# A value loop whose VectorE order is written out, with gathers issued five steps ahead

## The chip, the cores and the metric

The kernel runs on one core of a Trainium2 chip. The metric is device time in microseconds (us), as the median of three runs. Profiled spans come from one further execution.

## What is computed

The reference is one layer of a hybrid encoder block on 512 tokens of width 1024: a convolution branch and a windowed attention branch are gated, merged and added to x; then comes a retrieval layer over 16384 single-neuron experts, and a final norm. The change lies in the retrieval layer, so only that is shown, cut to what matters:

```python
for hc in four chunks of 128 tokens:                     # hc: (128, 1024), after RMSNorm
    q  = (hc @ w_query).reshape(128, 8, 2, 128)
    sc = einsum('thpd,pnd->thpn', q, sub_keys)
    vals, idx = top_k(sc, 16)                            # two half keys per head
    expert_idx, gate = top 16 of the 16 x 16 sums, softmax over them
    u   = expert_u[expert_idx]                           # 8 heads x 16 = 128 rows a token
    act = gelu(einsum('thkd,td->thk', u, hc))
    vv  = expert_v[expert_idx]
    y   = einsum('thk,thkd->td', gate * act, vv)
out = rmsnorm(x + y)
```

## The kernel before

The three later token chunks (384 tokens) are worked densely. For each of 128 blocks of 128 experts, `u_block(i)` (lines 491 to 506) loads a 512 KB block of transposed `expert_u` (tile `uraw`), splits it into a high and a low part (`uhi` on ScalarE, `ulo` on GpSimd, two halves a block, line 60), multiplies it with the tokens in 24 matmuls (`hps`, lines 65 to 67) and applies Gelu (line 504, tile `hb`). `v_block(i)` (lines 758 to 763) is the value side. It first calls `v_prep(i + 1)`, which prepares the next block: a load of `expert_v` (`vraw`, line 737, two buffers), its split (`vhl`: high half on ScalarE, low half on VectorE), the product of `hb` with the gates (line 747, VectorE, gates in `gt`, one load for four blocks), and the split of that product (`ph` on ScalarE, `pl` on VectorE, three buffers each). Then 18 matmuls add block i into six PSUM accumulators (`acc`).

Chunk 0 (128 tokens) is worked sparsely: its 128 chosen rows of `expert_u`, then its 128 rows of `expert_v`, are gathered one row per token by an indirect DMA from GpSimd's queue (`gather`, line 701, tile `row`, five buffers, 512 KB each). `step(c)` for c below 128 multiplies gathered rows of u with the tokens and sums (line 708); for c from 128 on it adds a weighted row of v to `yacc` (line 719). Each step is one long VectorE instruction.

The value loop (lines 815 to 824) weaves both. It runs i from 10 to 124. For i up to 91 an iteration has a v block, u block i + 36 and about 2.67 steps; from 92 on (33 iterations) no u block is left and an iteration has a v block and about 1.13 steps. These shares are the constants `R_BOTH` and `R_ONE`. The last three v blocks (125 to 127) follow the loop: blocks 126 and 127 are prepared, then the matmuls run token chunk by token chunk, each chunk followed by `finish`, which adds the residual, norms and stores. `finish(0)` takes `yacc` and stands just ahead of them (line 827).

Each engine works through its own queue in order. The order within a queue comes from the scheduler at build time, which simulates the program and takes, on each engine, what it holds ready, by program priority. Where `tc.manual_schedule` names an engine, that engine's queue keeps the program's order instead. Before the change it names GpSimd alone (line 815): its queue holds, per iteration, the two `ulo` of the u block and then the gathers of that iteration's steps. VectorE's order is the scheduler's. ScalarE, SyncE (which issues the loads) and TensorE are ordered by the scheduler in both kernels.

Of the kernel before, what the change touches and what calls it, by code (L numbers as in the profile page):

```python
# [27 lines left out]
NKEY = 128  # L28
# [7 lines left out]
VB, PB, VR, GB = 4, 3, 2, 5  # L36
UQ, UB = 2, 4
LAST = 3
# [8 lines left out]
def encoder_block(ctx, tc, x, xT, g1, w_in, taps, dwb, lng, lnb, w_pw, sink, w_o, w_out, g2, g2row,  # L47
# [443 lines left out]
    def u_block(i):  # L491
        raw = ust.tile([P, KD, P], F32, name="uraw", bufs=2)
        SP.dma_start(raw.rearrange("p k c -> p (k c)"), ut[i])
        ps = psh.tile([P, TB], F32, name="hps")
        for q in range(UQ):
            n = KD // UQ
            ks = slice(q * n, (q + 1) * n)
            hi = ust.tile([P, n, P], F32R, name="uhi", bufs=UB)
            lo = ust.tile([P, n, P], F32R, name="ulo", bufs=UB)
            split(hi, lo, raw[:, ks, :], POOL)  # L500
            mm3(ps, [(hi[:, k, :], lo[:, k, :]) for k in range(n)],
                [(h2_hi[:, q * n + k, P:], h2_lo[:, q * n + k, P:]) for k in range(n)], q == 0, q == UQ - 1)
        hb = hring.tile([P, TB], F32, name="hb")
        ACT.activation(hb, ps, AF.Gelu)  # L504
        hblk[i] = hb
# [193 lines left out]
    def gather(table, c):  # L699
        row = gath.tile([P, D], F32, name="row")  # L700
        POOL.indirect_dma_start(out=row, out_offset=None, in_=table,  # L701
                                in_offset=bass.IndirectOffsetOnAxis(ap=eidx[:, c:c + 1], axis=0))
        return row

    def step(c):
        if c < NKEY:
            row = gather(u, c)
            DVE.scalar_tensor_tensor(row, row, 1.0, h2tok, op0=OP.mult, op1=OP.mult,  # L708
                                     accum_out=dots[:, c:c + 1])
            if c == NKEY - 1:  # L710
                ACT.activation(dots, dots, AF.Gelu)
                DVE.tensor_tensor(dots, dots, gate_w, op=OP.mult)
        else:
            c -= NKEY
            row = gather(v, c)
            if c == 0:
                DVE.tensor_scalar(yacc, row, dots[:, 0:1], None, op0=OP.mult)
            else:
                DVE.scalar_tensor_tensor(yacc, row, dots[:, c:c + 1], yacc, op0=OP.mult, op1=OP.add)  # L719
# [38 lines left out]
    def v_block(i):  # L758
        v_prep(i + 1)
        for t in range(NB):  # L760
            for hf in range(2):
                v_mm(i, t, hf)
        prepped.pop(i)
# [48 lines left out]
    done, c = 0.0, 0  # L812
    both_n = NKEY - LEAD - NP
    unit = 2.0 * NKEY / (both_n * R_BOTH + (NKEY - NP - both_n) * R_ONE - 4)
    with tc.manual_schedule(engines={mybir.EngineType.Pool}):
        for i in range(NP, NKEY - LAST):
            v_block(i)
            both = i + LEAD < NKEY
            if both:
                u_block(i + LEAD)  # L820
            done += unit * (R_BOTH if both else R_ONE)
            while c < 2 * NKEY and (c < done or i == NKEY - LAST - 1):
                step(c)
                c += 1
    gfint = vst.tile([P, D], F32, name="h2tok", bufs=1)
    SP.dma_start(gfint, bcast(gfin, D))
# [76 lines left out]
```

## Time and profile before

| | us |
|---|---|
| median of three runs | 1776.07 |
| lowest and highest run | 1769.18 and 1780.47 |
| the profiled execution | 1779.59 |
| its span, first to last instruction | 1777.8 |
| busy: TensorE, VectorE, GpSimd, ScalarE | 1723.7, 1425.5, 945.5, 777.7 |
| mean granted TensorE clock | 0.989 of full |

The profiled execution is 1.8 us longer than its span, and 3.5 us longer than the median. Line numbers such as L60 are lines of the kernel; the helper `split` puts all its low parts on L60 and its high parts on L59, so they are told apart by tile. PE is TensorE's matmuls, PEld its weight loads, DVE VectorE, ACT ScalarE, POOL GpSimd, SP SyncE. "idle before" is the engine's idle time just ahead of an instruction and what ended it.

### The profile page before, as it was taken

Reading aid. Unit: us, or ns where it says so; the run is one execution under the profiler, and the core shown is the slowest. Engines: PE = TensorE matmul, PEld = TensorE weight load, DVE = VectorE, ACT = ScalarE, POOL = GpSimd, SP = SyncE. Lnnn points to the kernel's source line nnn. Section 1 sums busy time; section 2 is a strip of 40 time slices with the busy share of each in tenths; the row PEclk is TensorE's granted clock in tenths of the full one; section 3 lists DMA queues with packets and bytes.
Section 4 is the critical chain, followed back from the end, with each engine's and each line's share of the span. In section 5 each row is a group of like instructions: output and inputs, shape, how many; then the busy total and the mean of one; then the engine's idle time right before and its main releaser. Section 6 shows DMA issues by size and latency. Waiting matters only on the chain.

```text
span 1777.8 us, 25338 instructions
## 1 busy us (share of the span) xinstructions
PE 1723.7 (97%) x8843; PEld 1487.6 (84%) x8843; DVE 1425.5 (80%) x2523; ACT 777.7 (44%) x1386; POOL 945.5 (53%) x745
## 2 busy tenths in 40 slices
PE   7999999989999979999999999999999999998998
PEld 6888876668888878998999999999999988997786
DVE  7999967674437999999668888888878768898964
ACT  5333368972253336665433333333433332332343
POOL 6544420020135444445358888878876677786401
PEclk9999999999999989999999999999999999999999
DMA  4232210043243125987879998988997888899952
GB/s 160 98 102 97 95 39 33 13 148 101 83 149 105 45 65 162 285 259 245 311 256 312 328 317 307 328 320 316 319 326 278 314 303 294 304 329 333 357 204 93
DMA packets 158976, 379.44 MB, mean 213 GB/s; under 512 B 12592, under 2 KB 64832, under 8 KB 158848
## 3 DMA queue, kind: packets, MB, share of 16 engines
q1 hardware_dynamic: 120720, 241.73, 38.9%
q0 software_dynamic: 37120, 134.52, 22.0%
q10 hardware_dynamic: 1008, 1.58, 0.3%
q8 instruction: 69, 1.13, 0.3%
q14 instruction: 59, 0.48, 0.1%
HBM read 346.84 MB, written 30.93 MB: 212 GB/s over the span
## 4 chain that ended last, share of the span: by engine, by line
PE 63%; DVE 13%; DMA 12%; issue 6%; POOL 3%; ACT 2%; SPq 0%; ACTq 0%; POOLq 0%; DVEq 0%
PE mm L65 7%; PE mm L67 7%; PE mm L66 7%; PE acc L67 6%; PE acc L66 6%; PE acc L65 6%; PE hps L66 6%; PE hps L65 6%; PE hps L67 5%; DMA row<-in_v_dram,eidx 5%; DMA uraw<-in_ut_dram 3%; DMA vraw<-in_v_dram 2%; PE s L65 2%; POOL row L701 1%; PE s L66 1%
## 5 line engine op out<-in xcount | busy, mean ns | idle before, releaser
L60 POOL TENSOR_TENSOR ulo<-uraw,uhi 128x512 fp32r<-128x512 f32 x256 | 400.7, 1581 | 306.6 <-ACT uhi L59 278.7
L67 PE MATMUL hps<-big,ulo 128*128 128x384 f32 x1024 | 349.0, 341 | 3.6 <-POOL ulo L60 3.6
L65 PE MATMUL hps<-big,uhi 128*128 128x384 f32 x1024 | 348.8, 341 | 2.2 <-ACT hb L504 2.1
L66 PE MATMUL hps<-big,uhi 128*128 128x384 f32 x1024 | 347.5, 339 | 0.0
L67 PE MATMUL acc<-vhl,pl 128*128 128x512 f32 x768 | 301.7, 393 | 8.0 <-DVE pl L60 8.0
L65 PE MATMUL acc<-vhl,ph 128*128 128x512 f32 x768 | 301.3, 392 | 3.6 <-ACT vhl L59 3.5
L66 PE MATMUL acc<-vhl,ph 128*128 128x512 f32 x768 | 301.7, 393 | 0.9 <-DVE vhl L60 0.9
L60 POOL TENSOR_TENSOR wlo<-wraw,whi 128x512 fp32r<-128x512 f32 x120 | 160.8, 1344 | 176.4 <-ACT whi L59 153.6
L708 DVE SCALAR_TENSOR_TENSOR row<-row,h2tok 128x1024 f32<-128x1024 f32 x128 | 206.0, 1610 | 58.3 <-DMA row<-in_u_dram,eidx 56.5
L719 DVE SCALAR_TENSOR_TENSOR yacc<-row,dots,yacc 128x1024 f32<-128x1024 f32 x127 | 193.3, 1522 | 58.4 <-DMA row<-in_v_dram,eidx 58.2
L59 ACT ACTIVATE vhl<-vraw 128x1024 fp32r<-128x1024 f32 x128 | 135.5, 1059 | 230.5 <-DMA vraw<-in_v_dram 207.8
L59 ACT ACTIVATE uhi<-uraw 128x512 fp32r<-128x512 f32 x256 | 157.1, 631 | 167.0 <-PE hps L66 75.3
L65 PEld LDWEIGHTS hps<-big,uhi 128*128 128x128 f32 x1024 | 194.4, 190 | 6.4 <-ACT hb L504 2.4
L67 PEld LDWEIGHTS hps<-big,ulo 128*128 128x128 f32 x1024 | 194.3, 190 | 5.3 <-POOL ulo L60 5.3
L66 PEld LDWEIGHTS hps<-big,uhi 128*128 128x128 f32 x1024 | 194.9, 190 | 4.0
L701 POOL DMA_INDIRECT row<-in_u_dram,eidx x128 | 178.6, 1396 | 31.6 <-issue 25.8
L59 ACT ACTIVATE whi<-wraw 128x512 fp32r<-128x512 f32 x152 | 95.2, 631 | 209.9 <-PE mm L66 141.5
L701 POOL DMA_INDIRECT row<-in_v_dram,eidx x128 | 155.1, 1211 | 55.5 <-DVE yacc L719 31.1
L60 DVE TENSOR_TENSOR vhl<-vraw,vhl 128x1024 fp32r<-128x1024 f32 x128 | 162.7, 1271 | 24.4 <-ACT vhl L59 24.2
L67 PEld LDWEIGHTS acc<-vhl,pl 128*128 128x128 f32 x768 | 145.3, 189 | 41.4 <-DVE pl L60 10.5
L65 PE MATMUL mm<-big,whi 128*128 128x512 f32 x448 | 178.0, 397 | 0.4 <-DVE big L105 0.4
L66 PE MATMUL mm<-big,whi 128*128 128x512 f32 x448 | 176.4, 394 | 0.0
(243 smaller groups left out, 3073.3 us busy)
## 6 DMA issues: line engine op xcount, KB each, us to landing
uraw<-in_ut_dram SPq DMA_DIRECT2D x128, 512.0 KB
vraw<-in_v_dram SPq DMA_DIRECT2D x128, 512.0 KB
gates_dram<-st SPq DMA_DIRECT2D x12, 2048.0 KB
gt<-gates_dram SPq DMA_DIRECT2D x96, 256.0 KB
wraw<-in_w_in_dram SPq DMA_DIRECT2D x42, 512.0 KB
wraw<-in_w_query_dram SPq DMA_DIRECT2D x16, 512.0 KB
wraw<-in_w_o_dram SPq DMA_DIRECT2D x8, 512.0 KB
oraw<-in_w_out_dram SPq DMA_DIRECT2D x16, 256.0 KB
```

What stands on the lines that cost most here:

```text
L59: ACT.activation(hi, src, AF.Copy)
L60: lo_engine.tensor_tensor(lo, src, f(hi), op=OP.subtract)
L65: PE.matmul(ps, wh, mh, start=first and i == 0, stop=False)
L66: PE.matmul(ps, wh, ml, start=False, stop=False)
L67: PE.matmul(ps, wl, mh, start=False, stop=last and i == n - 1)
L701: POOL.indirect_dma_start(out=row, out_offset=None, in_=table, in_offset=bass.IndirectOffsetOnAxis(ap=eidx[:, c:c + 1], axis=0))
L708: DVE.scalar_tensor_tensor(row, row, 1.0, h2tok, op0=OP.mult, op1=OP.mult, accum_out=dots[:, c:c + 1])
L719: DVE.scalar_tensor_tensor(yacc, row, dots[:, c:c + 1], yacc, op0=OP.mult, op1=OP.add)
```

## The change

VectorE joins GpSimd in `manual_schedule`, so that in the loop both queues keep the program's order. The gather is taken out of `step`; a new function `fetch` issues it. Five gathers are issued ahead of the loop, and each step is followed by the gather of the step five later. The steps themselves are placed five later in the loop's count (`done - GB`, GB is 5), which leaves the gather of step c in the iteration where it stood.

```diff
+    rows = {}
+
+    def fetch(c):
+        if c < 2 * NKEY:
+            rows[c] = gather(u if c < NKEY else v, c % NKEY)
+
     def step(c):
+        row = rows.pop(c)
         if c < NKEY:
-            row = gather(u, c)
             DVE.scalar_tensor_tensor(row, row, 1.0, h2tok, op0=OP.mult, op1=OP.mult,
                                      accum_out=dots[:, c:c + 1])
...
         else:
             c -= NKEY
-            row = gather(v, c)
...
-    with tc.manual_schedule(engines={mybir.EngineType.Pool}):
+    with tc.manual_schedule(engines={mybir.EngineType.Pool, mybir.EngineType.DVE}):
+        for c in range(GB):
+            fetch(c)
+        c = 0
         for i in range(NP, NKEY - LAST):
             v_block(i)
             both = i + LEAD < NKEY
             if both:
                 u_block(i + LEAD)
             done += unit * (R_BOTH if both else R_ONE)
-            while c < 2 * NKEY and (c < done or i == NKEY - LAST - 1):
+            while c < 2 * NKEY and (c < done - GB or i == NKEY - LAST - 1):
                 step(c)
+                fetch(c + GB)
                 c += 1
```

## Rows read from the trace of the kernel before

**Rows 1.** Busy time by stretch: PE, PEld, DVE, ACT, POOL, then granted clock, DMA share, GB/s.
```profile
1200.00:1300.00 100.00, 100.00 (x507) 91.16 (x506) 88.71 (x102) 38.73 (x61) 86.23 (x59) 1.00 0.90 322
1400.00:1500.00 100.00, 97.11 (x481) 87.83 (x480) 75.84 (x63) 33.40 (x55) 74.45 (x54) 0.98 0.81 292
1606.00:1692.00 86.00, 78.28 (x335) 63.63 (x334) 77.39 (x78) 24.49 (x35) 46.91 (x39) 0.96 0.95 350
```

**Rows 2.** Timeline of ScalarE, a stretch with u blocks: start, duration, instruction, idle before.
```profile
1119.72 0.53 ACT L59 ACTIVATE ph<-hb 128x384 fp32r<-128x384 f32 x1 [2.98 <-PE acc L66]
1120.15 1.05 ACT L59 ACTIVATE vhl<-vraw 128x1024 fp32r<-128x1024 f32 x1
...
1128.02 0.53 ACT L59 ACTIVATE ph<-hb 128x384 fp32r<-128x384 f32 x1 [2.98 <-PE acc L66]
```

**Rows 3.** Timeline of ScalarE, after the last u block and the last step.
```profile
1721.07 0.53 ACT L59 ACTIVATE ph<-hb 128x384 fp32r<-128x384 f32 x1 [2.60 <-PE acc L66]
...
1725.15 0.53 ACT L59 ACTIVATE ph<-hb 128x384 fp32r<-128x384 f32 x1 [2.60 <-PE acc L66]
```

**Rows 4.** Timeline of TensorE around its longest wait in the loop.
```profile
1624.59 0.39 PE L65 MATMUL acc<-vhl,ph 128*128 128x512 f32 x1
1624.81 0.39 PE L66 MATMUL acc<-vhl,ph 128*128 128x512 f32 x1
1630.25 0.80 PE L67 MATMUL acc<-vhl,pl 128*128 128x512 f32 x1 [5.04 <-DVE pl L60]
...
1631.69 0.63 PE L67 MATMUL acc<-vhl,pl 128*128 128x512 f32 x1
1632.12 0.63 PE L65 MATMUL acc<-vhl,ph 128*128 128x512 f32 x1
```

**Rows 5.** Waits from 1400 to 1500 us: total us, times, longest.
```profile
ACT vhl L59 <- DMA vraw<-in_v_dram: 38.5, 8, 11.8
DVE yacc L719 <- DMA row<-in_v_dram,eidx: 24.1, 5, 7.5
...
PE hps L67 <- POOL ulo L60: 2.9, 2, 2.0
```

**Rows 6.** Waits from 1600 to 1700 us.
```profile
PE acc L67 <- DVE pl L60: 8.0, 5, 5.0
```

**Rows 7.** Timeline of VectorE around that wait.
```profile
1620.22 0.55 DVE L60 TENSOR_TENSOR pl<-hb,ph 128x384 fp32r<-128x384 f32 x1
...
1623.02 2.64 DVE L719 SCALAR_TENSOR_TENSOR yacc<-row,dots,yacc 128x1024 f32<-128x1024 f32 x2
...
1629.64 0.55 DVE L60 TENSOR_TENSOR pl<-hb,ph 128x384 fp32r<-128x384 f32 x1
```

**Rows 8.** Groups on VectorE from 1610 to 1692 us: count, busy us, mean ns, idle before.
```profile
L719 DVE SCALAR_TENSOR_TENSOR yacc<-row,dots,yacc 128x1024 f32<-128x1024 f32 x39 | 50.0, 1282 | 3.4 <-DMA row<-in_v_dram,eidx 3.3
L60 DVE TENSOR_TENSOR vhl<-vraw,vhl 128x1024 fp32r<-128x1024 f32 x16 | 19.6, 1222 | 5.2 <-ACT vhl L59 5.1
```

**Rows 9.** Instructions reading `eidx`: duration ns min/median/max, first and last start.
```profile
L701 POOL DMA_INDIRECT row<-in_u_dram,eidx x128: 937/1304/1990, 918.7 to 1311.2; - x128
...
L808 DVE SCALAR_TENSOR_TENSOR eidx<-ij x1: 293/293/293, 838.9 to 838.9; 128x128 int32<-128x128 f32 x1
```

**Rows 10.** Timeline of VectorE, a stretch with u blocks.
```profile
1121.57 1.22 DVE L60 TENSOR_TENSOR vhl<-vraw,vhl 128x1024 fp32r<-128x1024 f32 x1
1122.71 1.22 DVE L708 SCALAR_TENSOR_TENSOR row<-row,h2tok 128x1024 f32<-128x1024 f32 x1
...
1130.42 0.55 DVE L747 TENSOR_TENSOR hb<-hb,gt 128x384 f32<-128x384 f32 x1
```

**Rows 11.** Timeline of GpSimd: both `ulo` of one u block, unhindered.
```profile
1107.29 2.56 POOL L60 TENSOR_TENSOR ulo<-uraw,uhi 128x512 fp32r<-128x512 f32 x2
```

**Rows 12.** Chain that ended last, loads of `vraw`: start, us.
```profile
1342.64 4.41 DMA vraw<-in_v_dram
...
1645.64 7.55 DMA vraw<-in_v_dram
```

## The prediction

> **What bounds the kernel now.** I read the busy times by stretch first. In the loop's first part TensorE is busy without a gap (100.00 of 100 us at full granted clock, VectorE 88.71, GpSimd 86.23) [rows 1]. So the question is not how busy VectorE is, but what an order of VectorE can give to or take from TensorE. TensorE's pace is read off ScalarE, whose `ph` waits for the block of `acc` that frees its buffer: from one to the next it is 8.30 us with a u block [rows 2] and 4.08 us without [rows 3]. With 82 iterations of the first kind and 33 of the second, no order of VectorE makes these shorter.
>
> What can be won is therefore TensorE's idle time in the loop, and two stretches hold nearly all of it: 2.9 of 100 us near 1450 and 7.7 of 86 us after 1606, with a granted clock of 0.98 and 0.96 [rows 1]. If the clock falls to its lower level (1.2 of 2.4 GHz), 0.04 missing over 86 us means 6.9 us at half speed, so 3.4 us lost; 0.02 over 100 us means 2.0. The timeline shows that this follows a stall: matmuls that started 0.22 us apart before the 5.04 us wait start 0.43 apart after it [rows 4]. All that can be won is thus 2.9 + 2.0 + 7.7 + 3.4 = 16.0 us, under 1% of 1779.6 (17.8 us).
>
> The waits name the causes. Near 1450 VectorE stood up to 7.5 us at a step for its gather, with the next block's `vhl` queued behind; that held a buffer of `vraw`, ScalarE stood 11.8 us for the load, `uhi` and `ulo` came late behind it, and TensorE waited 2.9 us for `ulo` [rows 5]. After 1606 it waited 8.0 us for `pl` [rows 6]: in 9.4 us between two `pl` (1620.22 to 1629.64) VectorE's order holds steps out of proportion [rows 7]. Nothing paces the steps once the u blocks are gone: 39 steps beside 16 `vhl`, 2.4 a block [rows 8], where the program counts 1.13.
>
> **The change part by part.** *The gathers.* GpSimd's queue keeps its order: step c moves five later and its gather stays. Five buffers held five gathers before, too; the gather of c + 5 waits for step c in both kernels. So "five ahead" by itself moves no transfer. The first five are now ahead of `ulo` of block 46. Their index tile is written at 838.9 us, and the first gather of before started at 918.7 [rows 9], so they can land in time and cost nothing; if they held up `ulo`, five issues of 1.3 us would be 6.5, against a GpSimd with 14% idle [rows 1].
>
> *VectorE's order with u blocks.* Per iteration the queue holds `vhl`, the gate product, `pl` and 2.67 steps. A successor starts 0.08 us before the end of an instruction, so alone they take 1.14, 0.55, 0.47 and 2.67 x 1.14 = 3.04 us [rows 7, 10], 5.20 in all. New is a wait: `ph` is made from the gate product that stands just ahead of `pl`, so VectorE stands 0.53 us for ScalarE [rows 2], with `pl`, the steps and the next `vhl` behind it; before, the products ran far ahead. Today's busy share, with all that GpSimd disturbs, is 88.71% of 8.30 = 7.36 us [rows 1]. Adding the wait and the 0.08 of overlap that it breaks gives 7.97, under 8.30. From the other side, if `ulo` (2.56 us a block [rows 11]) never ran beside VectorE, 5.20 + 0.53 + 2.56 = 8.29. Bounds 5.7 and 8.3; I take 7.97, the measured load, so TensorE stays the bound. VectorE then waits at `pl` for the buffer, two blocks (8.2 us or more) ahead of need, and the slack that today is spent on gathers is spent there. That lead also covers ordinary jitter, so the stall near 1450 should go; since a late load can still start such a chain, I count half of its 4.9 us as coming back (2.5; bounds 0 and 4.9).
>
> The Trainium skill's page "SBUF — State Buffer" (Who interferes with whom) says that a VectorE instruction with two SBUF inputs and a reading GpSimd instruction lock each other out for a whole instruction. The trace agrees that something of the kind acts: alone the queue needs 5.20 of the 7.36 us in which it is busy. By that rule the bound is the 8.29 above, which leaves nothing to spare.
>
> *The last 33 iterations.* Steps are now paced. VectorE needs 1.14 + 0.55 + 0.53 + 0.47 + 1.13 x 1.20 = 4.05 us a block, against 4.08. The wait for `pl` after 1606 and its slow clock go: 11.1 us (7.7 + 3.4). But the next limit is near. `vraw` has two buffers, so the load of block n + 1 starts when `vhl` of n - 1 ends, and then come 4.41 to 7.55 us of load [rows 12], 1.05 on ScalarE [rows 2] and 1.22 of `vhl` [rows 8]: 6.7 to 9.8 us for two blocks, 3.3 to 4.9 a block. At the middle it is 4.13. Gathers fall to 1.13 a block, so loads should come no later than now; I take 4.2, because this and VectorE's 4.05 take turns at being late. Over 33 blocks that is 0.12 x 33 = 4 us, taken from the lead of 8.2 us; the bounds are 0 and (4.9 - 4.08) x 33 = 27.
>
> *The end.* Before, all steps were over by 1692 us, ahead of [rows 3]. Now the last iteration (i = 124) holds five steps (251 to 255), and blocks 126 and 127 are prepared behind them. With T the end of block 122's matmuls, `pl` of 125 is done at T + 1.0, the steps at T + 7.0 (5 x 1.20), block 126 (2.6 us) at T + 9.6, block 127 at T + 12.2. TensorE is through 123 and 124 at T + 8.2, needs 126 at T + 8.9 (three matmuls later) and waits 0.7, needs 127 at T + 10.3 and waits 1.9: 2.6 us, plus what is gone of the lead (4), so 6.6. Bounds: 0, if the scheduler puts the two blocks ahead of the steps, and 10.8 with no lead left.
>
> **Sum.** 1779.6 (the profiled execution: span 1777.8 and 1.8 around it) - 16.0 + 2.5 + 6.6 = 1772.7, say 1773. The median shown is 3.5 us under that execution, so it would give 1769; I keep 1773, as the runs spread by 11 us. Own range of this case: 1763 (all 16 won, nothing lost) to 1783 (half of it won and the end at its bound).
>
> **Rivals.**
> *ScalarE's order puts the load's split first* (slower). If in the last 33 iterations ScalarE's queue has the high half of block n + 1 ahead of `ph` of n, then `ph`, `pl`, a step and the next `vhl` all wait for a load: 5.98 (the middle) + 1.05 + 0.53 + 0.47 + 1.36 + 1.22 = 10.6 us for two blocks, 5.30 a block. It decides from 4.08 on. 33 x 1.22 = 40, less the lead 8.2, plus 10.8 at the end, less 13.5 won: 1779.6 + 29 = 1809. For it: in [rows 2] the high half stands right beside `ph`, and `ph` now becomes ready later. Against: there `ph` comes first.
> *VectorE becomes the bound with u blocks* (slower). From 8.30 on; at 8.6, 82 x 0.3 = 25, less the lead 8.2, plus 10.8, less 11.1: 1796. For it: 8.29 above. Against: 7.97, and TensorE's lead of two blocks.
> *The stall only moves.* What is won after 1606 is lost at the end, where five steps, two blocks and the first `finish` meet, with the slow clock behind them (0.2 us for each matmul at half speed [rows 4]): 1778. The change would then not do what it says.
> *TensorE has room.* If its 100% hid slack of 8.84% (weight loads 91.16 of 100 us [rows 1]), 82 x 8.30 x 0.088 = 60 us might be open: 1720. Against it, matmuls follow each other at a fixed spacing with full clock. The Trainium skill ("Perfetto Trace Analysis", Identifying the Most-Contended Engine) would judge by weight loads rather than matmul time; nothing in this trace shows VectorE's order reaching that remainder.
>
> **How the numbers follow.** Forecast 0.62, ScalarE's order 0.13, VectorE the bound 0.08, the stall only moves 0.10, room on TensorE 0.02, unnamed 0.05. About 1%, or 18 us, is what a measurement of this kernel can tell from no change. Faster by more needs TensorE's room or a lucky median: 0.04. Slower by more: most of the first two rivals and of the unnamed, 0.23. Within: 0.73. The range runs from 1760 (everything won, on the median's scale) to 1802, which takes in VectorE as the bound and the milder part of ScalarE's order.
>
> **What would show it.** Right: no TensorE wait above 2 us between 920 and 1690; step and `vhl` about 1.13 to 1 in the last 33 iterations; `ph` spaced 8.30 and 4.08; VectorE waiting for `ph` in place of gathers; a wait for blocks 126 and 127 near the end. Wrong: a spacing above 8.4, or above 4.4 in the last 33 iterations; ScalarE long idle for `vraw` ahead of `ph`; gathers that VectorE still stands for by tens of us.

## The result, and the profile after

Four runs of the changed kernel have a median of 1794.89 us (1787.75 to 1798.87), against 1772.87 for four runs of the kernel before beside them (1776.07 above is the median of three of these). The ratio on record, which is not the quotient of the two medians, is 1.0105, 95% interval 1.007 to 1.0139. The change is slower, by about 1% and clear of the interval. The profiled execution took 1794.63 us, its span is 1792.9.

The first view is the busy time by stretch of the changed kernel (PE, PEld, DVE, ACT, POOL, granted clock, DMA share, GB/s); its first three rows answer to [rows 1].

```profile
1200.00:1300.00 100.00, 100.00 (x508) 91.24 (x507) 85.24 (x103) 36.55 (x60) 83.79 (x57) 1.00 0.88 319
1400.00:1500.00 100.00, 100.00 (x508) 91.22 (x508) 85.41 (x68) 36.31 (x60) 83.98 (x57) 1.00 0.88 317
1606.00:1692.00 86.00, 83.36 (x368) 67.98 (x367) 59.87 (x71) 27.78 (x37) 31.48 (x19) 1.00 0.72 259
1692.00:1758.00 66.00, 59.21 (x236) 45.07 (x234) 46.99 (x56) 18.11 (x24) 24.77 (x15) 0.95 0.74 260
1758.00:1793.00 35.00, 20.80 (x72) 15.62 (x72) 23.49 (x36) 15.31 (x32) 9.53 (x7) 0.84 0.49 176
```

Near 1450 TensorE now waits for nothing, and the big hole after 1606 has shrunk to 2.6 us. What is lost comes later: 6.8 of 66 us from 1692 on and 14.2 of the last 35 (the end of the program among them), at a clock of 0.95 and then 0.84. VectorE is no bound there (59.87 of 86 us, where it had 77.39), nor are the transfers (share 0.72, 259 GB/s, where [rows 1] has 350). The last `hps` matmul starts at 1610.4 us in both kernels, so the loss lies wholly behind it: to the last `acc` matmul it is 159.4 us in the kernel before and 172.4 in the changed one, and the end behind that takes 10.0 us in place of 8.0. That 1610.4 stands in both is a balance: in the changed kernel the stall near 1450 is gone, but its index tile is written 2.2 us later (841.1, [rows 9] has 838.9) and TensorE has a new wait of 2.8 us near 865.

The waits of the changed kernel from 1606 to 1793 us (total, times, longest) answer to [rows 6].

```profile
ACT vhl L59 <- DMA vraw<-in_v_dram: 78.0, 27, 5.5
DVE pl L60 <- ACT ph L59: 49.4, 31, 4.9
...
PE acc L65 <- ACT ph L59: 12.0, 11, 2.5
...
PE acc L67 <- DVE pl L60: 1.2, 1, 1.2
```

The 8.0 us for `pl` are down to 1.2. In their place TensorE stands eleven times for `ph`, at the start of a block, VectorE thirty-one times for `ph`, and ScalarE for the load of `vraw`. Why these three belong together is in the chain of waits of the changed kernel, here one turn of it (start, us, what):

```profile
1693.57 1.15 DVE vhl L60
...
1694.77 6.33 DMA vraw<-in_v_dram
...
1701.19 0.04 ACT vhl L59
1701.23 0.92 issue
1702.15 0.52 ACT ph L59
...
1702.69 0.04 DVE pl L60
...
1703.16 1.29 DVE yacc L724
...
1705.68 1.23 DVE vhl L60
...
1706.96 4.61 DMA vraw<-in_v_dram
```

VectorE's `vhl` frees a load buffer, the load of the block two later runs, ScalarE makes that block's high half, and only then `ph`, of the block before it; `pl`, the steps and the next `vhl` follow, which starts the next load. This turn, 1694.77 to 1706.96, is 12.2 us for two blocks; it has two steps and is longer than the mean. Nothing in `ph` needs the load: it is behind it in ScalarE's queue. The timelines of ScalarE and VectorE of the changed kernel say the same (start, duration, instruction, idle before):

```profile
1701.19 1.06 ACT L59 ACTIVATE vhl<-vraw 128x1024 fp32r<-128x1024 f32 x1 [5.27 <-DMA vraw<-in_v_dram]
1702.15 0.51 ACT L59 ACTIVATE ph<-hb 128x384 fp32r<-128x384 f32 x1
```

```profile
1698.76 0.56 DVE L752 TENSOR_TENSOR hb<-hb,gt 128x384 f32<-128x384 f32 x1
1702.69 0.56 DVE L60 TENSOR_TENSOR pl<-hb,ph 128x384 fp32r<-128x384 f32 x1 [3.37 <-ACT ph L59]
```

The product that `ph` is made from was done at 1699.3; `ph` started at 1702.15, right behind a high half that stood 5.27 us for its load. Counted by block over the trace: from block 99 to 125, 27 blocks, ScalarE has the high half of n + 1 ahead of `ph` of n. In the kernel before it is so in no block of the loop. From `pl` of block 99 (1632.9) to that of block 124 (1760.2) it is 5.09 us a block, where TensorE needs 4.08 [rows 3].

VectorE's groups from 1610 to 1692 us answer to [rows 8]: the steps are paced as the program counts them, 18 beside 16 `vhl` in place of 39.

```profile
L724 DVE SCALAR_TENSOR_TENSOR yacc<-row,dots,yacc 128x1024 f32<-128x1024 f32 x18 | 23.0, 1280 | 0.1
L60 DVE TENSOR_TENSOR vhl<-vraw,vhl 128x1024 fp32r<-128x1024 f32 x16 | 19.5, 1219 | 0.0
```

### The profile page after: what moved, and what is told of

It reads as the page before. It is cut to its first block, busy times and chain, and to the rows that moved or that the text cites. A ratio compares the mean times of both kernels' runs of the same rounds, so it can differ in the third digit from the quotient of the medians.

```text
span 1792.9 us, 25110 instructions
## 1 busy us (share of the span) xinstructions
PE 1731.3 (97%) x8843; PEld 1490.0 (83%) x8843; DVE 1413.1 (79%) x2523; ACT 771.4 (43%) x1386; POOL 963.7 (54%) x745
## 4 chain that ended last, share of the span: by engine, by line
PE 77%; DVE 13%; DMA 5%; ACT 2%; issue 2%; POOL 1%; POOLq 0%; ACTq 0%; SPq 0%; DVEq 0%
PE hps L65 8%; PE hps L67 8%; PE hps L66 8%; PE acc L66 7%; PE acc L65 7%; PE acc L67 7%; PE mm L65 7%; PE mm L67 7%; PE mm L66 7%; DMA vraw<-in_v_dram 4%; PE s L65 2%; PE s L66 1%; DVE yacc L724 1%; PE s L67 1%; DVE oij L673 1%
## 5 line engine op out<-in xcount | busy, mean ns | idle before, releaser
L60 POOL TENSOR_TENSOR ulo<-uraw,uhi 128x512 fp32r<-128x512 f32 x256 | 406.5, 1596 | 295.8 <-ACT uhi L59 284.4
L701 POOL DMA_INDIRECT row<-in_v_dram,eidx x128 | 180.4, 1409 | 125.4 <-DVE yacc L724 101.3
L59 ACT ACTIVATE ph<-hb 128x384 fp32r<-128x384 f32 (+1 forms) x132 | 67.1, 512 | 387.3 <-DVE hb L752 326.9
L724 DVE SCALAR_TENSOR_TENSOR yacc<-row,dots,yacc 128x1024 f32<-128x1024 f32 x127 | 199.9, 1574 | 15.9 <-DMA row<-in_v_dram,eidx 14.1
L60 DVE TENSOR_TENSOR vhl<-vraw,vhl 128x1024 fp32r<-128x1024 f32 x128 | 198.3, 1550 | 15.7 <-ACT vhl L59 15.7
L60 DVE TENSOR_TENSOR pl<-hb,ph 128x384 fp32r<-128x384 f32 (+1 forms) x132 | 73.9, 562 | 142.9 <-ACT ph L59 142.9
L65 PEld LDWEIGHTS acc<-vhl,ph 128*128 128x128 f32 x768 | 146.1, 190 | 47.8 <-ACT ph L59 16.6
L701 POOL DMA_INDIRECT row<-in_u_dram,eidx x128 | 166.3, 1300 | 31.5 <-issue 26.3
L65 PE MATMUL mm<-big,whi 128*128 128x512 f32 x448 | 178.0, 397 | 0.3 <-DVE big L105 0.3
```

The costliest lines, as they stand in the source:

```text
L59: ACT.activation(hi, src, AF.Copy)
L60: lo_engine.tensor_tensor(lo, src, f(hi), op=OP.subtract)
L65: PE.matmul(ps, wh, mh, start=first and i == 0, stop=False)
```

## The experiments

The theories: A, ScalarE's order, as above; B, the chain of loads over two buffers, with VectorE's own 4.05 us a block; C, the steps left for the end. Twelve kernels ran; times are medians. They ran in four sittings, and each ratio is against the kernel before in the same sitting, on the same chip: 1775.95 us for the first four rows, 1773.94 for the next four, 1775.11 for the next three, 1775.87 for the last (the first and the third sitting had the same chip). Between rows of different sittings the ratios are to be compared, and ratios whose intervals overlap are not told apart. "Spacing" is the mean distance of `pl` from block 99 to 124 in the one trace of each kernel.

| run | us | ratio, 95% interval | spacing |
|---|---|---|---|
| scalare_late | 1780.65 | 1.0018 (1.0006 to 1.003) | 4.42 |
| gate_one_ahead | 1771.66 | 0.9976 (0.9961 to 0.9992) | 4.14 |
| vectore_free_late | 1779.2 | 1.0016 (1.0 to 1.0031) | 4.06 |
| fetch_alone | 1775.0 | 0.9991 (0.9974 to 1.0008) | 3.95 |
| late_four_buffers | 1774.98 | 1.0012 (0.9998 to 1.0026) | 4.21 |
| gate_ahead_order_reversed | 1795.17 | 1.0111 (1.0081 to 1.0141) | 5.16 |
| gate_ahead_late_fill | 1768.54 | 0.9972 (0.9958 to 0.9986) | 4.14 |
| gate_ahead_paced_end | 1767.19 | 0.9958 (0.9939 to 0.9976) | 4.07 |
| all_three | 1763.99 | 0.9939 (0.9916 to 0.9962) | 4.15 |
| scalare_late_paced | 1778.46 | 1.0018 (1.0003 to 1.0033) | 4.43 |
| order_alone | 2108.86 | 1.1889 (1.1852 to 1.1927) | 4.95 |
| order_alone_gate_ahead | 2090.29 | 1.1795 (1.1757 to 1.1832) | 4.10 |

(A spacing below 4.08 is a VectorE that still catches up after it was late, or widens its lead.)

**scalare_late.** The loop is cut in two; in the last 33 iterations ScalarE's queue keeps the program's order too, which has `ph` of n ahead of the high half of n + 1.

```diff
-        for i in range(NP, NKEY - LAST):
+        for i in range(NP, NKEY - LEAD):
...
+    with tc.manual_schedule(engines={mybir.EngineType.Pool, mybir.EngineType.DVE, mybir.EngineType.Activation}):
+        for i in range(NKEY - LEAD, NKEY - LAST):
```

> Only ScalarE's queue in the last 33 iterations changes: it takes the program's order there, so that ph of block n stands ahead of the high half of block n + 1; VectorE's and GpSimd's order and the pacing of steps stay those of the change. Theory A (ScalarE's order: ph, pl, step and the next vhl hang behind a load) expects that pl of blocks 99 to 125, now 5.07 us apart, comes 4.1 to 4.3 us apart, that TensorE's loss before 1760 us goes from some 16 us to under 4, and a time near 1778. Theory B (two buffers of vraw, gate loads among them and VectorE's 4.05 us a block are too tight whatever ScalarE's order) expects less than 5 us of change and a time over 1788. Theory C (only the steps and preparations left for the end) expects the loss before 1760 to stay.

Measured: 1780.65 us, 14.2 under the changed kernel, spacing 4.42 in place of 5.09. The queue of TensorE is that of the changed kernel, SyncE's and VectorE's are but for a few places; in ScalarE's one reversed block is left, 125. Here the high half starts right behind `ph`, and it is `ph` that waits, for its own product (timeline of ScalarE in this kernel):

```profile
1703.23 0.53 ACT L59 ACTIVATE ph<-hb 128x384 fp32r<-128x384 f32 x1 [2.56 <-DVE hb L752]
1703.66 1.05 ACT L59 ACTIVATE vhl<-vraw 128x1024 fp32r<-128x1024 f32 x1
1707.26 0.52 ACT L59 ACTIVATE ph<-hb 128x384 fp32r<-128x384 f32 x1 [2.55 <-DVE hb L752]
```

So ScalarE's order is most of the loss, and not all: 4.42 is over the 4.1 to 4.3 that I expected and over 4.08, and the last blocks lose time.

**gate_one_ahead.** The gate product of a block is taken out of `v_prep` and stands one block earlier in VectorE's queue. ScalarE's order is left to the scheduler.

```diff
...
             v_block(i)
+            v_gate(i + 2)
...
```

> The gate product of block n + 2 is computed one iteration earlier, right behind the preparation of block n + 1, so that ph no longer waits for the instruction just ahead of pl. VectorE keeps the program's order; the number of instructions is the same. Theory A expects ScalarE's queue to have ph ahead of the next high half again, a pl spacing of 4.1 to 4.3 us in the last 33 iterations and a time of 1772 to 1777. Theory B expects the load's chain to stay: spacing 4.6 or more and a time over 1785.

Measured: 1771.66 us, under the kernel before by a little (0.9976) and under the changed one by 23.2, spacing 4.14. With the product early the scheduler put no high half ahead of the `ph` before it, in any block. VectorE no longer stands between the product and `pl` (timeline of VectorE in this kernel):

```profile
1691.97 1.22 DVE L60 TENSOR_TENSOR vhl<-vraw,vhl 128x1024 fp32r<-128x1024 f32 x1
1693.11 0.55 DVE L60 TENSOR_TENSOR pl<-hb,ph 128x384 fp32r<-128x384 f32 x1
1693.57 0.55 DVE L746 TENSOR_TENSOR hb<-hb,gt 128x384 f32<-128x384 f32 x1
1694.04 1.28 DVE L724 SCALAR_TENSOR_TENSOR yacc<-row,dots,yacc 128x1024 f32<-128x1024 f32 x1
```

Two things changed at once here, the order and the wait, so the next run parts them.

**gate_ahead_order_reversed.** The same kernel, with the high half of n + 1 written ahead of `ph` of n from about block 99 on, and ScalarE held to the program's order there.

```diff
...
-        split(hi, lo, raw, DVE)
...
+        hi, lo, raw = v_high(i)
+        DVE.tensor_tensor(lo, raw, f(hi), op=OP.subtract)
+        if i > NKEY - LEAD + 6:
+            v_high(i + 1)
...
```

> The kernel with the gate product one block earlier (1771.66 us), but in the last iterations with ScalarE's order as in the changed kernel: the high half of block n + 1 ahead of ph of n. VectorE's order and the early product stay. Theory A (ScalarE's order is the cause): the spacing at pl goes from 4.14 back to about 5.1 us, 25 blocks x 0.9 = 23 less some 6 us of lead: 1786 to 1796 us. Rival D (what cures is that ph no longer waits for a product made just ahead of it; the order is only a companion): the spacing stays below 4.4 and the time at 1770 to 1776.

Measured: 1795.17 us, spacing 5.16, the same 27 blocks reversed as in the changed kernel. The order alone brings the whole loss back, with the product early; rival D falls. The waits of this kernel from 1606 to 1793 us:

```profile
ACT vhl L755 <- DMA vraw<-in_v_dram: 93.7, 25, 6.5
DVE pl L60 <- ACT ph L59: 48.8, 23, 4.9
...
PE acc L65 <- ACT ph L59: 13.0, 10, 3.5
```

**vectore_free_late.** In the last 33 iterations VectorE's order is the scheduler's again.

```diff
+    with tc.manual_schedule(engines={mybir.EngineType.Pool}):
+        for i in range(NKEY - LEAD, NKEY - LAST):
```

> VectorE's order is the program's up to iteration 91 and the scheduler's in the last 33. Theories A and B both expect the loss of the last stretch to go back to what it was before (some 10 us there, as steps run unpaced), and the gain near 1450 us (5 us) to stay: 1768 to 1773. If the first 82 iterations were themselves slower under the program's order, it would stay over 1780.

Measured: 1779.2 us, a miss: I expected 1768 to 1773. ScalarE's order is right, but the old hole is back. Busy times of this kernel from 1606 to 1692 us, then one of its waits from 1606 to 1720:

```profile
1606.00:1692.00 86.00, 79.96 (x340) 64.82 (x338) 79.08 (x91) 24.72 (x34) 40.22 (x35) 0.96 0.98 362
```

```profile
PE acc L67 <- DVE pl L60: 7.1, 6, 4.3
```

That is [rows 1] and [rows 6] over again (78.28 and 0.96; 8.0 us). This speaks for VectorE's written order winning there what the forecast said, and for the changed kernel paying it away on ScalarE. It rests on one trace of each kernel, and the next run shows that the hole can be small under the scheduler's order, too.

**fetch_alone.** Gathers five ahead, GpSimd alone held to the program's order.

```diff
-    with tc.manual_schedule(engines={mybir.EngineType.Pool, mybir.EngineType.DVE}):
+    with tc.manual_schedule(engines={mybir.EngineType.Pool}):
```

> The gathers are issued five steps ahead and the steps are counted five later, but VectorE's order stays with the scheduler. Theories A and B put the loss on VectorE's order and expect a time within 5 us of the kernel before (1768 to 1778). If the five steps left for the end were the cause (theory C), it would be 1785 or more.

Measured: 1775.0 us, no difference from the kernel before. Without VectorE's order the gathers' distance does nothing to the time that can be measured. Its trace is another, though. One of its waits from 1606 to 1720 us, beside the 8.0 of [rows 6]:

```profile
PE acc L67 <- DVE pl L60: 1.9, 5, 0.8
```

VectorE has 38 steps beside 16 `vhl` from 1610 to 1692 us here, as out of proportion as before, but TensorE comes to that stretch 4.3 us later (its last `hps` matmul starts at 1614.7), among other things by a wait of 3.0 us for `hb` near 868. One reading is that what TensorE loses earlier it need not wait for here; nothing tests it.

**late_four_buffers.** The kernel of scalare_late; from block 97 on every second load goes into an idle buffer of `uraw`.

```diff
-        raw = vst.tile([P, D], F32, name="vraw", bufs=VR)
+        if i > NKEY - LEAD + 3 and i % 2:
+            raw = ust.tile([P, KD, P], F32, name="uraw", bufs=2).rearrange("p k c -> p (k c)")
+        else:
+            raw = vst.tile([P, D], F32, name="vraw", bufs=VR)
```

> The kernel with ScalarE's order written out in the last iterations (1780.65 us; blocks 99 to 124 follow each other 4.42 us apart at pl), and from block 97 on every second load of expert_v goes into a buffer of uraw, idle by then: four load buffers in place of two. Theory B (the rest of the loss is the load chain over two buffers): the spacing falls to 4.08 to 4.2, the lead of 6.3 us that block 99 still has is kept to block 120, and the loss at the end shrinks with it: 1772 to 1776 us. Theory C (the rest is the five steps and two blocks at the end, whatever the loads do): the spacing may fall, the time doesn't: 1779 to 1782. If VectorE itself is the limit there (my 4.05 us a block was too low), the spacing stays at 4.4 and the time at 1780.

Measured: 1774.98 us, spacing 4.21. The median is as theory B had it, but the ratio (1.0012) is not told apart from that of scalare_late (1.0018). The traces do tell them apart: `pl` of block 120 starts 4.7 us ahead of its first matmul, where scalare_late has 0.4. Of the 0.34 us by which 4.42 is over 4.08, 0.21 was the chain of loads. The rest is VectorE, which no longer waits for any load of `expert_v` (timeline of VectorE in this kernel):

```profile
1703.82 1.22 DVE L60 TENSOR_TENSOR vhl<-uraw,vhl 128x1024 fp32r<-128x1024 f32 x1
1704.95 0.55 DVE L755 TENSOR_TENSOR hb<-hb,gt 128x384 f32<-128x384 f32 x1
1706.18 0.56 DVE L60 TENSOR_TENSOR pl<-hb,ph 128x384 fp32r<-128x384 f32 x1 [0.67 <-ACT ph L59]
1706.65 1.28 DVE L724 SCALAR_TENSOR_TENSOR yacc<-row,dots,yacc 128x1024 f32<-128x1024 f32 x1
1707.85 1.22 DVE L60 TENSOR_TENSOR vhl<-vraw,vhl 128x1024 fp32r<-128x1024 f32 x1
```

A block with one step takes 4.03 us (1703.82 to 1707.85); every eighth block or so has a second step, 1.3 us more, 0.16 a block: 4.19.

**scalare_late_paced.** The kernel of scalare_late, with the steps' count scaled so that the last step falls some three iterations before the loop's end.

```diff
-    unit = 2.0 * NKEY / (both_n * R_BOTH + (NKEY - NP - both_n) * R_ONE - 4)
+    unit = (2.0 * NKEY + GB) / (both_n * R_BOTH + (NKEY - NP - both_n) * R_ONE - 4)
```

> The kernel with ScalarE's order written out in the last iterations (1780.65 us), and the steps ended three iterations before the loop's end; two load buffers, gate product where the change has it. Theory C (the five steps at the end): the waits from 1748 to 1758 (8.8 us and slow clock) go: 1770 to 1774. Theory B (the load chain at 4.42 us a block): the lead of 6.3 us at block 99 is still used up by block 115 to 120, and 2 us or more a few blocks later are lost: 1774 to 1778.

Measured: 1778.46 us, spacing 4.43: just over theory B's upper end. `pl` of block 99 is 5.1 us ahead of its first matmul, that of block 115 0.7, that of 120 0.3. While 4.43 stands over 4.08, an end free of steps lowers the median by 2.2 us and leaves the ratio where it was (1.0018 in both): no gain that can be told.

**gate_ahead_paced_end, gate_ahead_late_fill.** Two kernels, each with one edit on gate_one_ahead. The first has the scaled count of steps just shown. The second issues the first five gathers with the first iterations' steps:

```diff
-        for c in range(GB):
-            fetch(c)
+        c, nf = 0, 0
...
+            while nf < GB and nf < done:
+                fetch(nf)
+                nf += 1
```

> The kernel with the gate product one block earlier, and the steps' count scaled so that the last step falls some three iterations ahead of the loop's end, as in the kernel before (the numerator 256 becomes 261): no five steps at the last iteration. Theory C (steps left for the end cost what blocks 126 and 127 wait): TensorE's 4 us of waits from 1740 to 1750 go and blocks 125 to 127 end 12 us after the start of 125's matmuls: 1766 to 1769 us. Rival: the norm of chunk 0, which then stands among the last blocks, or VectorE's 2% more load takes the same time: 1770 to 1774.

> The kernel with the gate product one block earlier, and the first five gathers issued with the first iterations' steps instead of ahead of the loop. If those five gathers (2.5 MB at 840 to 865 us) are what makes TensorE wait 3.1 us for hb near 862 us, where the kernel before has no such wait: that wait goes, 1767 to 1769.5 us. If the wait has another cause (the scheduler's order ahead of the loop): the wait stays, 1771 to 1772.5.

Measured: 1767.19 and 1768.54 us. The medians are 4.5 and 3.1 under gate_one_ahead, but that ran in another sitting. By the ratios (0.9958 and 0.9972, against 0.9976) it is 3.2 and 0.7 us, and the intervals overlap, so neither time is told apart from it. The traces show more. With the paced end TensorE waits nowhere in the last blocks, where gate_one_ahead has two waits, of 1.45 and 1.17 us, and a clock of 0.97 from 1692 to 1758 (busy times of the kernel with the paced end):

```profile
1606.00:1692.00 86.00, 86.00 (x386) 71.97 (x385) 69.19 (x82) 31.38 (x41) 30.60 (x22) 1.00 0.85 302
1692.00:1758.00 66.00, 65.72 (x290) 54.10 (x289) 55.77 (x72) 29.60 (x48) 24.02 (x15) 1.00 0.68 246
```

The late fill takes away a wait that the changed kernel has, and the kernel before has not (waits of the changed kernel, 842 to 907 us):

```profile
ACT ph L59 <- DVE hb L752: 4.7, 1, 4.7
...
PE hps L65 <- ACT hb L504: 2.8, 1, 2.8
DVE hb L752 <- DMA gt<-gates_dram: 2.7, 1, 2.7
```

Five gathers (2.6 MB) beside the loads of the loop's start make other loads late: from 838 to 870 us a load of `gt` took 10.0 us (median) to land in the changed kernel and 6.0 with the late fill. The product and `ph` wait for `gt`; Gelu, behind them in ScalarE's queue, also stands behind two high halves whose loads of `vraw` are late (2.6 and 1.3 us of wait), and at last TensorE waits. fetch_alone, where VectorE's order is the scheduler's but the five gathers are issued ahead as well, has the same wait, 3.0 us, so it comes from the gathers. With the late fill the last `hps` matmul starts at 1605.3 in place of 1608.5.

**all_three.**

> The changed kernel with three edits: the gate product one block earlier, the first five gathers issued with the first iterations' steps, the last step three iterations before the loop's end. If the three losses are separate (3.1 us of wait near 862, 4 us at 1740 to 1750, both seen alone), they add: 1771.66 - 3.1 - 4.5 = 1764, with TensorE waiting nowhere over 1 us between 845 and 1755. If one hides another, 1766 to 1768.

Measured: 1763.99 us, 0.9939 of the kernel before and 1.7% under the changed kernel. Here the comparison with gate_one_ahead is on the same chip: its six runs (up to 1765.29) all lie under the ten of gate_one_ahead (from 1767.45), so the two edits together do win time, 7.7 us by the medians and 6.6 by the ratios. That the losses add is not shown to the microsecond: 1771.66 - 3.1 - 4.5 = 1764.1 takes its terms from medians of another sitting, and by the ratios the two edits alone give 3.9. Of TensorE's waits two are left between 845 and 1755 us, 0.6 and 0.3 us near 1742.

**order_alone, order_alone_gate_ahead.** VectorE's order by the program, but each gather where the kernel before has it, just ahead of its own step; then the same with the gate product one block earlier. The first is this one edit on the kernel before:

```diff
-    with tc.manual_schedule(engines={mybir.EngineType.Pool}):
+    with tc.manual_schedule(engines={mybir.EngineType.Pool, mybir.EngineType.DVE}):
```

> VectorE's order given by the program, and the gathers where the kernel before issues them, each just ahead of its step in the program; no five steps at the end. ScalarE's order here has the high half of block n + 1 ahead of ph of n in both parts of the loop. Theory A (that order costs 5.1 us a block without u blocks, nothing with them, as 8.30 is longer): 1785 to 1795, somewhat under the changed kernel since the end is free of steps. Rival E (the gathers' distance is what VectorE's order needs: with a step right behind its own gather VectorE stands for each one): VectorE waits for row by hundreds of us, TensorE below 100 of 100 us with u blocks, over 1810.

> VectorE's order with each step right behind its own gather, as in the run at 2108.86 us, and the gate product one block earlier, which brings ScalarE's order to that of the kernel before in the whole loop. If the 330 us come from steps that stand for their own gather (rival E): VectorE still waits some 35 of 100 us for row with u blocks and the time stays over 2000 us. If they come from ScalarE's reversed order in the 80 blocks with u blocks: 1765 to 1790 us.

Measured: 2108.86 and 2090.29 us. In the first, ScalarE's order is reversed in 80 blocks with u blocks as well; in the second in none, and the time stays over 2000. Waits and busy times of the second kernel from 1200 to 1300 us:

```profile
DVE row L708 <- DMA row<-in_u_dram,eidx: 39.4, 14, 6.6
```

```profile
1200.00:1300.00 100.00, 79.20 (x344) 66.94 (x343) 55.44 (x66) 26.46 (x44) 57.61 (x40) 0.91 0.62 221
```

Rival E holds: a step right behind its own gather stands for it, with `vhl` and the next block behind it, and TensorE falls to 79.20 of 100 us. The five steps of distance are what makes a written order of VectorE bearable; no other distance was tried.

## Why the prediction was wrong, point by point

The forecast was 1773 us, 7 under the profiled execution of before. The changed kernel came out slower: 1794.89 us, inside the stated range (1760 to 1802) only in the part that it kept for the first two rivals.

**What bounds the kernel** held. TensorE is busy for 100 of 100 us from 907 to 1606 us in the changed kernel, and no run here was faster there. By the Trainium skill ("Perfetto Trace Analysis", Identifying the Most-Contended Engine) weight loads would be the measure of room left; PEld stayed at 91.2 of 100 us in the changed kernel, as in [rows 1], and nothing that ran here got at the remainder.

**The two stalls** went, as forecast: 100.00 of 100 us near 1450 and 1.2 us for `pl`. Half of the first was not given back; in its place came 2.8 us near 865.

**The first five gathers** were costed at nothing, since they could land in time. They did; what they delayed was other loads, of `gt` and of `vraw`. TensorE waited 2.8 us for it, a wait that fetch_alone shares and that goes with the late fill; what it costs in the time alone is not told from noise. I had looked at their own due time, not at whose transfers they share the engines with.

**VectorE with u blocks** held in the size: busy 85.24 and waiting 7.8 us for `ph` in 100 us, 12.05 blocks, so 7.7 us a block against my 7.97. It also stays below the 8.29 that I had for VectorE and `ulo` never running at once. By the Trainium skill ("SBUF — State Buffer", Who interferes with whom) a VectorE instruction with two SBUF inputs contends with a GpSimd instruction that reads SBUF; 7.7 does not speak against that, since `ulo` can run while VectorE waits. I was wrong on where the slack goes. VectorE does not wait at `pl` for a buffer that TensorE holds: `ph` waits for its product, and what is left of the slack still goes to gathers (waits of the changed kernel, 1200 to 1300 us):

```profile
ACT ph L59 <- DVE hb L752: 49.3, 12, 5.0
...
DVE pl L60 <- ACT ph L59: 7.8, 12, 0.7
...
DVE row L714 <- DMA row<-in_u_dram,eidx: 6.9, 3, 3.3
```

**The last 33 iterations** are where it failed. The step is "I take 4.2" us a block for load chain and VectorE. It rested on ScalarE's queue as it stood, with `ph` ahead of the load's split ([rows 2], "there `ph` comes first"), and that order was not the change's to keep: only VectorE's queue is given by the program, ScalarE's is made anew around it. With the order reversed it measured 5.09. That was my first rival, at a chance of 0.13; its mechanism is shown from both sides, by scalare_late (-14.2 us) and gate_ahead_order_reversed (+23.5 us). Its price was too high, 1809 for 1795: it counted 33 blocks at 5.30, and there were 27 at some 5.09, as the order turns only at block 99. Why at 99 stays open.

Even with the order of before the term was mis-sized: 4.42 (scalare_late), of which 0.21 is the load chain and the rest VectorE at 4.19 in place of my 4.05. I had the wait for `ph` at its bare 0.53; it is 0.67, and that is the difference.

**The end**: forecast 6.6 us, 2.6 of waits and 4 of lead lost. With the order cured (gate_one_ahead) TensorE waits 1.45 + 1.17 = 2.6 us there, and the paced end takes that away; in the time it is 4.5 us by medians of two sittings and 3.2 by the ratios, not told from nothing. The order that I assumed was wrong. I had blocks 126 and 127 prepared behind all five steps; in the changed kernel they stand among them, and the last step follows the last `pl` (timeline of VectorE):

```profile
1770.30 0.56 DVE L60 TENSOR_TENSOR pl<-hb,ph 128x384 fp32r<-128x384 f32 x1
...
1772.56 1.28 DVE L724 SCALAR_TENSOR_TENSOR yacc<-row,dots,yacc 128x1024 f32<-128x1024 f32 x1
```

So that the 2.6 us agree is in part luck. That the end behind the last matmul took 10.0 us in the changed kernel and 8.1 in gate_one_ahead was not taken apart further.

**The sum.** The changed kernel less its separate losses is 1794.9 - 23.2 (the early product: order and wait for `ph`) - 3.1 - 4.5 = 1764, near what I gave to "everything won" (1763). Trace against trace that is 16.3 us (1779.59 to 1763.25), what the prediction counted; but the traced execution of before was one of the slower ones, and by the ratio of all_three the gain is 11 us (7 to 15). So there is a gain to be had; its size was read off one slow execution. Why the scheduler turned ScalarE's order is only argued: `ph` becomes ready later when its product stands just ahead of `pl`, so at that moment it holds the next high half ready first. That an early product keeps the order speaks for it.

## What to carry to other kernels

Whoever fixes the order of one queue has changed the others, too, if these are made by a scheduler: read the new order of each engine that feeds the fixed one, block by block, before a spacing is forecast from the old trace. An in-order queue that holds a load's consumer ahead of an instruction that needs no load ties two independent chains together; producing the second one's input a block earlier cut the tie here (23 us). A written order also needs its distances: gathers five steps ahead were worth over 300 us to it, and nothing that could be measured without it.

## What was not expected of the hardware

Loads were waited for while the DMA engines were not full: from 1630 to 1740 us of the changed kernel a 512 KB load took 3.1 to 7.7 us from issue to landing (median 4.0) at a DMA share of 0.73. That points at the time of the single load rather than at the bandwidth; no run parts the two. And some of the short stalls at block boundaries lowered the granted clock for the matmuls behind them (0.95 from 1692 to 1758 us); in the timeline of TensorE of the changed kernel these stand 0.23 apart before a wait of 2.13 us and up to 0.47 after it, as in [rows 4].

```profile
1699.96 0.39 PE L66 MATMUL acc<-vhl,ph 128*128 128x512 f32 x1
1700.19 0.39 PE L67 MATMUL acc<-vhl,pl 128*128 128x512 f32 x1
1702.71 0.50 PE L65 MATMUL acc<-vhl,ph 128*128 128x512 f32 x1 [2.13 <-ACT ph L59]
...
1703.43 0.67 PE L67 MATMUL acc<-vhl,pl 128*128 128x512 f32 x1
1703.90 0.63 PE L65 MATMUL acc<-vhl,ph 128*128 128x512 f32 x1
```

Not every stall did: from 1606 to 1692, with 2.6 us of waits up to 1.42 long, the clock was 1.00.
